# HGRN scores: the near halves of both directions in one 128x128 matmul per chunk, and the far half with doubled queries

## The chip, the cores and the metric

The kernel runs on one core of one Trainium2 chip. The metric is device time in microseconds (us) from start to end of one execution; lower is better. Five engines work side by side, each on its own list of instructions in order: PE (matmul, with its weight loads shown apart as PEld), DVE (vector operations), ACT (activation functions and copies), POOL and SP (which here issues the DMA transfers). They wait for one another through semaphores.

## The reference, cut to what matters

The reference is a two-layer backbone over 512 latent tokens and 256 context tokens of width 1024. Its first layer has a bidirectional HGRN2 mixer: a gated linear recurrence, run forward and backward, with 8 heads of 128 features. Within a chunk each direction computes scores between queries and keys, masked to what lies behind, and multiplies them with the values:

```python
b = jnp.cumsum(logf, axis=-2)
q_in = q * jnp.exp(b)
k_in = k * jnp.exp(-b)
scores = jnp.where(lower, jnp.einsum('nbhtd,nbhsd->nbhts', q_in, k_in), 0.0)
o_intra = jnp.einsum('nbhts,nbhse->nbhte', scores, v)
```

`f`, and so `b`, differs for the two directions; the backward direction is the same on flipped tokens. The two directions' outputs are added. The rest of the program (modulation, feed-forward halves, gated chunk MLP) is not touched by the change.

## The kernel before, in words

Weights stream from HBM in units of 128x1024; ACT and DVE split each into two parts (`split`, L95 on ACT and L96 on DVE, tile `w`), and each product of the large projections is three matmuls (L107, L108, L109). The units pass through buffers that come free as PE works on, so each split is released by PE's progress.

The HGRN stage loops over heads `h`, with the work on head `h - 1` put between the projections of head `h`. For each head PE makes: the forget projection of direction 0 (`psfl`, then `psfc` for the context tokens, L649 and L651), that of direction 1, the query projection `psq` of head `h`, and the gate projection `psq` of head `h - 1`. All of these are 24 matmuls of 512 or 256 columns. ACT and DVE turn each forget projection into the key tile `X` (Exp, Ln, Ln on ACT, L657 to L660; subtract, add, cumulative sum on DVE, L661 to L666; six references on L679; Exp on L680) and the decay tile `B` (L682, L683). The query projection goes through three ACT passes (L636 to L638) and one DVE product (L639). Then `queries` (L688) multiplies `B` of direction 0 and of direction 1 with the queries, one DVE instruction each: after it `B` is the query operand `Q` of that direction.

For head `h - 1` PE transposes keys (`ptk`, L694; ACT copies them to `kT`, L696), makes the states (`pkc`, `pkl`) and the scores. `scores` works on chunks of 128 tokens, keys on partitions, four chunks per direction. A 128x128 score block has a near half of 64 queries that see only 64 keys, and a far half of 64 queries that see all 128. So each chunk takes two matmuls: 64 keys by 64 queries (L707) and 128 keys by 64 queries (L708). DVE copies the allowed entries to the score tile `sT` with two predicated copies per direction (L711, L712). `outputs` adds the score tiles of the two directions (`ssum`, L760) and multiplies with the values (`po`, L764 to L766); the output is normalised (`on`), transposed (`pto`, L782), and multiplied with the gate.

The tile framework reorders instructions of one engine when it builds the program, so the order in the code is not exactly that of an engine; once built, each engine's order is fixed. Before the change the scores of direction 0 stand behind the next head's first forget projection and the transposes, those of direction 1 behind its second one.

Of the kernel before, what the change touches and what calls it, by code (L numbers as in the profile page):

```python
# [42 lines left out]
def backbone_kernel(  # L43
# [72 lines left out]
    def silu_row(pool, c):  # L116
        """silu of a conditioning vector, on every partition."""
        s = pool.tile([P, D], F32, name=f"srow_{c}")
        nc.sync.dma_start(s, cond[CI_OF[c]].partition_broadcast(P))
        nc.scalar.activation(s, s, AF.Silu)  # L120
        return s

    def mod_dot(pool, dst, w, s):
        """Sums of the halves of the products, so that no sum grows long."""
        n = D // 2
        for i in range(2):
            c = slice(i * n, (i + 1) * n)
            junk = pool.tile([P, n], BF16, tag="junk", name="junk", bufs=2)
            nc.vector.scalar_tensor_tensor(junk, w[:, c], 1.0, s[:, c], ALU.mult, ALU.mult, dst[:, i : i + 1])  # L129
# [63 lines left out]
    class OutPhase:  # L193
        """y = h @ w_out by token tiles, z = alpha x + gate y, its LayerNorm, and the next operand.

        x comes with its factor alpha, but for the first one (scaled=False)."""
# [45 lines left out]
        def store(self):  # L242
            """alpha times the LayerNorm's full result, for the next residual."""
# [40 lines left out]
        def operand(self, p, kb):  # L284
            """Two feature tiles of the next operand, for a pair of token tiles."""
# [88 lines left out]
    class Phase:  # L374
        """What the boundary before a phase may already start."""

        urgent, later = True, iter(())  # whether the residual's store is made at once, and what is put off
# [4 lines left out]
        @staticmethod  # L382
        def share(i, n):
            """Of n parts: two before the first operand step, the rest once the others are on their way."""
            return {0: range(2), 4: range(2, n)}.get(i, ())

        def ahead(self, i):
            """Work that needs nothing of this boundary, before its i-th operand step."""
# [4 lines left out]
    class FeedIn(Phase):  # L393
        """gate and up projections of a half-FFN, features on partitions."""
# [44 lines left out]
    class FeedContext(FeedIn):  # L439
        """The same of the context, whose operand is there before the latents'."""  # L440
# [15 lines left out]
    class HgrnValues(Phase):  # L456
        """First half of the token-major value projection, its latent tokens."""
# [33 lines left out]
    # ================= layer 0 =================  # L491
# [5 lines left out]
    with tc.tile_pool(name="hp", bufs=1) as hp, tc.tile_pool(name="modp", bufs=1) as modp:  # L497
        nc.scalar.preload_act_table(AF.Silu)
        srow = {"x": silu_row(modp, "x")}
        # x (1 + scale) + shift, features on partitions, a feature tile at a time  # L500
        f0 = FeedIn(0, 0, xm, NT, 6)
        with tc.tile_pool(name="first", bufs=1) as fp:
# [24 lines left out]
            for k in range(KD):  # L527
# [5 lines left out]
                # one feature tile behind, so that the next one's operand is on its way meanwhile  # L533
# [42 lines left out]
    with tc.tile_pool(name="hgo", bufs=1) as hgo:  # L576
        hts = [hgo.tile([P, 2, T], F32R, name=f"ht{h}") for h in range(NH)]
        with tc.tile_pool(name="hg", bufs=1) as hg:
# [37 lines left out]
            # values, tokens on partitions  # L616
# [13 lines left out]
            def proj_silu(h, idx, tag):  # L630
                """x sigmoid(x), the sigmoid as exp(-ln(1 + exp(-x)))."""
# [12 lines left out]

            def proj_forget(h, d):
                """Logit x: with e = exp(-x), f = (1 + lb e) / (1 + e) and 1 - f = (1 - lb) exp(-x) / (1 + e)."""
# [5 lines left out]
                r, i = Dir(), d * NH + h  # L652
                X = hg.tile([P, SEG * P], F32, tag="X", name="X", bufs=3)
                nc.vector.tensor_scalar(X[:, :T], ps, LOGIT_MIN, None, ALU.max)
                nc.vector.tensor_scalar(X[:, T:], psc[:, :TC], LOGIT_MIN, None, ALU.max)
                B = hg.tile([P, SEG * P], F32, tag="B", name="B", bufs=4)
# [6 lines left out]
                # cumulative log-decay within chunks; keys and queries relative to the middle of a latent  # L663
                # chunk, the keys of the context relative to the end of theirs
                st = 1 if d == 0 else -1
                nc.vector.tensor_tensor_scan(B[:, ::st], resets[d][:, ::st], B[:, ::st], 0.0, ALU.mult, ALU.add)  # L666
                B3 = B.rearrange("p (s t) -> p s t", t=P)
# [12 lines left out]
                nc.scalar.activation(X, X, AF.Exp, scale=-1.0, bias=lnoml[:, i : i + 1])  # L680
                Q = B3[:, :NT, :]
# [20 lines left out]
            def scores(d, r):  # L702
                """Masked scores, keys on partitions."""
                psc3 = bank("pssc").rearrange("p (s t) -> p s t", t=P)
                near, far = (slice(0, H), slice(H, P)) if d == 0 else (slice(H, P), slice(0, H))
                for s in range(NT):
                    nc.tensor.matmul(psc3[near, s, near], r.kk[:, s, near], r.Q[:, s, near], start=True, stop=True)  # L707
                    nc.tensor.matmul(psc3[:, s, far], r.kk[:, s, :], r.Q[:, s, far], start=True, stop=True)  # L708
                sT = sts[d]
                mk = mask[d].bitcast(I32).broadcast_to([P, NT, P])  # L710
                nc.vector.copy_predicated(sT[near], mk[near], psc3[near])  # L711
                nc.vector.copy_predicated(sT[far, :, far], mk[far, :, far], psc3[far, :, far])  # L712
# [22 lines left out]
            def latent_states(h, d, r, kT):  # L735
# [7 lines left out]
                for i, s in enumerate(order):  # L743
# [6 lines left out]
                    S1 = hg.tile([P, P], F32, tag="S1", name="S1", bufs=2)  # L750
# [42 lines left out]
            for h in range(NH + 1):  # L793
                if h < NH:
                    n0, last = proj_forget(h, 0)
                else:
                    op.lead(0, 1)
# [3 lines left out]
                if prev:  # L801
                    r0, r1 = prev
                    kTc = transposed([r.kk[:, NT + s, :] for r in prev for s in range(NTC)])
                    kT0 = transposed([r0.kk[:, s, :] for s in lat_order(0)[:-1]])
                    scores(0, r0)
# [4 lines left out]
                if prev:  # L810
# [3 lines left out]
                    scores(1, r1)  # L814
# [25 lines left out]
    with tc.tile_pool(name="hp2", bufs=1) as hp, tc.tile_pool(name="modp2", bufs=1) as modp, bpools() as bp:  # L840
# [16 lines left out]
        class GateIn(Phase):  # L857
            """Token-major half of the chunk MLP's projection, its first group."""
# [118 lines left out]
def _feature_units(w):  # L977
    """(D, n * 128) -> (n, 128, D // 128 * 128): features by 128, contraction rows on partitions."""
    k, n = w.shape
    return w.reshape(k // P, P, n // P, P).transpose(2, 1, 0, 3).reshape(n // P, P, k)  # L980


def _row_units(w, block):
    """(k, n) -> (n // block, k // 256, 128, 2 * block): two contraction tiles of a block of columns."""
# [67 lines left out]
```

## Time and profile before

| | |
|---|---|
| time, median of 3 runs | 2554.14 us (2553.33 to 2558.38) |
| span of the profiled execution | 2559.4 us, 5.3 us (0.2%) above that median |
| PE busy | 2511.2 us, 98% of the span |
| DVE, ACT busy | 1561.4 us (61%), 887.5 us (35%) |
| mean granted PE clock | 0.994 |
| first forget projection to last head's output | 642.5 to 973 us |

The page gives no time of the profiled execution beside its span, so sums are made against the span, and differences are carried over to the median. A row of the timeline has the start in us from the start of the span, the duration in us, the engine, the line, the operation, output and input tiles with their shapes, and how often the instruction follows itself; brackets hold the idle time of that engine just before, and what ended it. Matmuls overlap in the pipeline, so their cost in a stream is read from start to start, not from their durations. A row of the table by stretches has the stretch, its length, the busy time of each engine with its instruction count, then the granted PE clock (1.00 is full), the DMA share and the GB/s.

### The profile page before, as it was taken

Reading aid. Unit: us, or ns where it says so; the run is one execution under the profiler, and the core shown is the slowest. Engines: PE = TensorE matmul, PEld = TensorE weight load, DVE = VectorE, ACT = ScalarE, POOL = GpSimd, SP = SyncE. Lnnn points to the kernel's source line nnn. Section 1 sums busy time; section 2 is a strip of 40 time slices with the busy share of each in tenths; the row PEclk is TensorE's granted clock in tenths of the full one; section 3 lists DMA queues with packets and bytes.
Section 4 is the critical chain, followed back from the end, with each engine's and each line's share of the span. In section 5 each row is a group of like instructions: output and inputs, shape, how many; then the busy total and the mean of one; then the engine's idle time right before and its main releaser. Section 6 shows DMA issues by size and latency. Waiting matters only on the chain.

```text
span 2559.4 us, 32071 instructions
## 1 busy us (share of the span) xinstructions
PE 2511.2 (98%) x12591; PEld 2142.1 (84%) x12591; DVE 1561.4 (61%) x2773; ACT 887.5 (35%) x1210; POOL 45.1 (2%) x80
## 2 busy tenths in 40 slices
PE   7999999999999999999899999999999999999998
PEld 5888889988888888888678888888998888888887
DVE  7987568472888876766766522357467446632255
ACT  4222335462544433321233322343332233422232
POOL 0000000000000000000000000000000000000001
PEclk9999999999999999999999999999999999999999
DMA  8878326551211113788832522222533222432221
GB/s 324 294 260 279 128 95 227 191 188 50 75 65 52 50 58 116 263 289 275 268 127 87 181 99 97 93 95 96 191 124 105 82 99 91 172 109 98 99 91 58
DMA packets 111000, 367.18 MB, mean 143 GB/s; under 512 B 12744, under 2 KB 16000, under 8 KB 110848
## 3 DMA queue, kind: packets, MB, share of 16 engines
q1 hardware_dynamic: 110848, 365.13, 41.5%
q8 instruction: 98, 1.61, 0.3%
q14 instruction: 54, 0.44, 0.1%
HBM read 352.47 MB, written 12.61 MB: 143 GB/s over the span
## 4 chain that ended last, share of the span: by engine, by line
PE 85%; DMA 7%; DVE 5%; POOL 1%; issue 1%; ACT 0%; SPq 0%; DVEq 0%; POOLq 0%; ACTq 0%
PE psf L108 11%; PE psf L109 11%; PE psf L107 11%; PE y L107 8%; PE y L109 8%; PE y L108 8%; DMA mraw<-in_mod_w 7%; DVE junk L129 2%; PE pscv L109 2%; PE pscv L108 2%; PE pscu L108 2%; PE pscu L107 2%; PE pscu L109 2%; PE pscv L107 2%; PE psfl L107 1%; PE psq L109 1%
## 5 line engine op out<-in xcount | busy, mean ns | idle before, releaser
L96 DVE TENSOR_TENSOR w<-raw,w 128x1024 fp32r<-128x1024 f32 (+1 forms) x458 | 550.1, 1203 | 338.1 <-ACT w L95 335.5
L95 ACT ACTIVATE w<-raw 128x1024 fp32r<-128x1024 f32 (+1 forms) x458 | 473.1, 1039 | 437.7 <-PE psf L109 199.5
L107 PE MATMUL psf<-xm,w 128*128 128x512 f32 (+1 forms) x1504 | 566.8, 379 | 18.2 <-ACT xm L95 17.7
L108 PE MATMUL psf<-xm,w 128*128 128x512 f32 (+1 forms) x1504 | 568.7, 378 | 2.1 <-DVE xm L96 2.1
L109 PE MATMUL psf<-xm,w 128*128 128x512 f32 (+1 forms) x1504 | 568.0, 378 | 1.5 <-DVE w L96 1.5
L109 PE MATMUL y<-w,hs 128*128 128x512 f32 x984 | 387.4, 394 | 14.3 <-DVE hs L96 14.3
L107 PE MATMUL y<-w,hs 128*128 128x512 f32 x984 | 388.1, 394 | 0.0
L108 PE MATMUL y<-w,hs 128*128 128x512 f32 x984 | 387.5, 394 | 0.0
L107 PEld LDWEIGHTS psf<-xm,w 128*128 128x128 f32 x1504 | 284.2, 190 | 71.5 <-ACT xm L95 18.8
L108 PEld LDWEIGHTS psf<-xm,w 128*128 128x128 f32 x1504 | 286.0, 190 | 54.7 <-DVE xm L96 3.5
L109 PEld LDWEIGHTS psf<-xm,w 128*128 128x128 f32 x1504 | 285.9, 190 | 53.9 <-DVE w L96 2.9
L96 DVE TENSOR_TENSOR hs<-h,hs 128x512 fp32r<-128x512 f32 (+1 forms) x220 | 138.6, 636 | 170.4 <-ACT hs L95 170.2
L109 PEld LDWEIGHTS y<-w,hs 128*128 128x128 f32 x984 | 185.7, 189 | 56.3 <-DVE hs L96 14.8
L95 ACT ACTIVATE hs<-h 128x512 fp32r<-128x512 f32 (+1 forms) x220 | 129.1, 588 | 289.2 <-PE y L109 260.0
L129 DVE SCALAR_TENSOR_TENSOR junk<-mraw,srow_x 128x512 bf16<-128x512 f32 x256 | 167.5, 688 | 87.7 <-DMA mraw<-in_mod_w 87.0
L107 PEld LDWEIGHTS y<-w,hs 128*128 128x128 f32 x984 | 185.8, 189 | 41.9 <-ACT hs L95 0.2
L108 PEld LDWEIGHTS y<-w,hs 128*128 128x128 f32 x984 | 185.9, 189 | 40.6
L417 ACT ACTIVATE silu<-psf 128x512 f32<-128x512 f32 (+1 forms) x110 | 60.8, 552 | 424.2 <-PE psf L109 241.7
L419 DVE TENSOR_TENSOR h<-psf,silu 128x512 f32<-128x512 f32 (+1 forms) x110 | 69.7, 634 | 101.7 <-PE psf L109 99.7
L107 PE MATMUL psf<-xmc,w 128*128 128x256 f32 x352 | 99.8, 284 | 0.0
L109 PE MATMUL psf<-xmc,w 128*128 128x256 f32 x352 | 99.7, 283 | 0.0
L108 PE MATMUL psf<-xmc,w 128*128 128x256 f32 x352 | 99.7, 283 | 0.0
(202 smaller groups left out, 3216.4 us busy)
## 6 DMA issues: line engine op xcount, KB each, us to landing
raw<-in_ffn_w_in SPq DMA_DIRECT2D x220, 512.0 KB, 3.6
mraw<-in_mod_w SPq DMA_DIRECT2D x144, 512.0 KB, 4.5
raw<-in_ffn_w_out SPq DMA_DIRECT2D x110, 512.0 KB, 3.2
raw<-in_hg_wf SPq DMA_DIRECT2D x32, 512.0 KB, 3.2
raw<-in_cm_wv SPq DMA_DIRECT2D x32, 384.0 KB, 3.1
raw<-in_cm_wu SPq DMA_DIRECT2D x24, 512.0 KB, 3.3
raw<-in_cm_w_out SPq DMA_DIRECT2D x24, 512.0 KB, 3.2
x<-x SPq DMA_DIRECT2D x40, 256.0 KB, 2.4
```

The costliest lines, as they stand in the source:

```text
L95: nc.scalar.activation(dst_hi, src, AF.Copy)
L96: return nc.vector.tensor_tensor(dst_lo, src, dst_hi.bitcast(F32), ALU.subtract)
L107: nc.tensor.matmul(ps, ah, bh, start=start, stop=False)
L108: nc.tensor.matmul(ps, ah, bl, start=False, stop=False)
L109: return nc.tensor.matmul(ps, al, bh, start=False, stop=stop)
L129: nc.vector.scalar_tensor_tensor(junk, w[:, c], 1.0, s[:, c], ALU.mult, ALU.mult, dst[:, i : i + 1])
L417: nc.scalar.activation(s[:, :n], psg[:, :n], AF.Silu)
L419: nc.vector.tensor_tensor(h[:, :n], psu[:, :n], s[:, :n], ALU.mult)
```

## The change

The two tiles `B` of one head become one tile of two rows, so that one access pattern can take 64 queries of direction 0 and 64 of direction 1 for a chunk. The near keys of both directions are copied side by side into a new tile `kkn` (one ACT copy per direction). `near_scores` multiplies both at once, 128 keys by 128 queries; of its result the two diagonal blocks of 64x64 are used, one for each direction, with one predicated copy each. `far_scores` keeps 128 keys by the 64 far queries, but reads those queries twice, as 128 columns, and uses the first half of the result. `near_scores` is called at the start of the next head's turn, ahead of its first forget projection; `far_scores` stands where `scores` stood. Tile `S1` has one buffer instead of two.

```diff
+            both = {}
+
+            def pair():
+
+                both = hg.tile([P, 2, SEG * P], F32, tag="B", name="B", bufs=2)
+                rows = both[:, 0, :]
+                near = bass.AP(
+                    tensor=rows.tensor, offset=rows.offset,
+                    ap=[rows.ap[0], [SEG * P + H, 2], [P, NT], [1, H]],
+                )
+                kkn = hg.tile([P, NT, 2, H], F32, tag="kkn", name="kkn", bufs=1)
+                return (both[:, 0, :], both[:, 1, :]), near, kkn
+
             def proj_forget(h, d):
...
+                if d == 0:
+                    both[h] = pair()
...
-                B = hg.tile([P, SEG * P], F32, tag="B", name="B", bufs=4)
+                Bs, r.Qn, r.kkn = both[h]
+                B = Bs[d]
...
                 nc.scalar.activation(X, X, AF.Exp, scale=-1.0, bias=lnoml[:, i : i + 1])
+                near = slice(0, H) if d == 0 else slice(H, P)
+                nc.scalar.activation(r.kkn[:, :, d, :], X3[:, :NT, near], AF.Copy)
...
-            def scores(d, r):
...
-                psc3 = bank("pssc").rearrange("p (s t) -> p s t", t=P)
-                near, far = (slice(0, H), slice(H, P)) if d == 0 else (slice(H, P), slice(0, H))
+            def near_scores(r):
+
+                ps = bank("pssn").rearrange("p (s t) -> p s t", t=P)
                 for s in range(NT):
-                    nc.tensor.matmul(psc3[near, s, near], r.kk[:, s, near], r.Q[:, s, near], start=True, stop=True)
-                    nc.tensor.matmul(psc3[:, s, far], r.kk[:, s, :], r.Q[:, s, far], start=True, stop=True)
-                sT = sts[d]
+                    nc.tensor.matmul(ps[:, s, :], r.kkn[:, s].rearrange("p d t -> p (d t)"), r.Qn[:, :, s, :], start=True, stop=True)
+                for d, n in ((0, slice(0, H)), (1, slice(H, P))):
+                    mk = mask[d].bitcast(I32).broadcast_to([P, NT, P])
+                    nc.vector.copy_predicated(sts[d][n, :, n], mk[n, :, n], ps[n, :, n])
+
+            def far_scores(d, r):
+
+                ps = bank("pssc").rearrange("p (s i t) -> p s i t", i=2, t=H)
+                far = slice(H, P) if d == 0 else slice(0, H)
+                for s in range(NT):
+                    q = r.Q[:, s, far].unsqueeze(1).broadcast_to([P, 2, H])
+                    nc.tensor.matmul(ps[:, s], r.kk[:, s, :], q, start=True, stop=True)
                 mk = mask[d].bitcast(I32).broadcast_to([P, NT, P])
-                nc.vector.copy_predicated(sT[near], mk[near], psc3[near])
-                nc.vector.copy_predicated(sT[far, :, far], mk[far, :, far], psc3[far, :, far])
+                nc.vector.copy_predicated(sts[d][:, :, far], mk[:, :, far], ps[:, :, 0, :])
...
-                    S1 = hg.tile([P, P], F32, tag="S1", name="S1", bufs=2)
+                    S1 = hg.tile([P, P], F32, tag="S1", name="S1", bufs=1)
...
             for h in range(NH + 1):
+                if prev:
+                    r0, r1 = prev
+                    near_scores(r0)
...
-                    scores(0, r0)
+                    far_scores(0, r0)
...
-                    scores(1, r1)
+                    far_scores(1, r1)
```

The built program differs on PE, DVE and ACT. In the pieces below, taken from a head in the middle of the loop, the line numbers are those of the kernel named.

PE, where the gate projection (`psq`) ends and the next head's first forget projection (`psfl`) begins. Before:

```order
L107 MATMUL psq<-xm,w 128x512
L108 MATMUL psq<-xm,w 128x512
L109 MATMUL psq<-xm,w 128x512
L107 MATMUL psfl<-xm,w 128x512
L108 MATMUL psfl<-xm,w 128x512
L109 MATMUL psfl<-xm,w 128x512
```

The change:

```order
L107 MATMUL psq<-xm,w 128x512
L108 MATMUL psq<-xm,w 128x512
L109 MATMUL psq<-xm,w 128x512
L724 MATMUL pssn<-B,kkn 128x128 x4
L107 MATMUL psfl<-xm,w 128x512
L108 MATMUL psfl<-xm,w 128x512
L109 MATMUL psfl<-xm,w 128x512
```

The four near matmuls (`pssn`) stand between the two projections. For the first head there is no gate projection of an earlier head, and they stand right behind the query projection. The first `po` matmuls of `outputs` follow eight `psfl` matmuls later (ten before).

DVE, around the products with the queries: `q` is the query product, `S`, `Sc` and the numbered `S_` tiles belong to the recurrent states. Before, from the query product on:

```order
L639 TENSOR_TENSOR q<-psq,q 128x512
L752 SCALAR_TENSOR_TENSOR S<-pkl,se,S_7940 128x128
L688 TENSOR_TENSOR B<-B,q 128x512
L745 TENSOR_SCALAR Sc<-S,se 128x128
L751 TENSOR_SCALAR S_7946<-S,se 128x128
L688 TENSOR_TENSOR B<-B,q 128x512
L752 SCALAR_TENSOR_TENSOR S<-pkl,se,S_7946 128x128
L760 TENSOR_TENSOR ssum<-sT_5377,sT_5378 128x512
L745 TENSOR_SCALAR Sc<-S,se 128x128
L96 TENSOR_TENSOR w<-raw,w 128x1024
```

The change, from the sum of the score tiles on:

```order
L785 TENSOR_TENSOR ssum<-sT_5377,sT_5378 128x512
L770 TENSOR_SCALAR Sc<-S,se 128x128
L776 TENSOR_SCALAR S_7544<-S,se 128x128
L777 SCALAR_TENSOR_TENSOR S<-pkl,se,S_7544 128x128
L770 TENSOR_SCALAR Sc<-S,se 128x128 x2
L776 TENSOR_SCALAR S_7562<-S,se 128x128
L96 TENSOR_TENSOR w<-raw,w 128x1024
L777 SCALAR_TENSOR_TENSOR S<-pkl,se,S_7562 128x128
L639 TENSOR_TENSOR q<-psq,q 128x512
L770 TENSOR_SCALAR Sc<-S,se 128x128
L776 TENSOR_SCALAR S_7568<-S,se 128x128
L706 TENSOR_TENSOR B<-B,q 128x512
```

The sum `ssum` and one split of a weight unit (L96) moved from behind the two query products of `B` to ahead of `q`; the second product of `B` follows two rows later. The near halves' predicated copies (L727) stand some rows further on, behind the gate product.

ACT, where a forget projection is finished. Before:

```order
L675 ACTIVATE se<-sm 128x14
L680 ACTIVATE X<-X,lnoml 128x768
L683 ACTIVATE B<-B 128x512
L95 ACTIVATE w<-raw 128x1024
L657 ACTIVATE B<-X 128x768
```

The change:

```order
L691 ACTIVATE se<-sm 128x14
L696 ACTIVATE X<-X,lnoml 128x768
L701 ACTIVATE B<-B 128x512
L698 ACTIVATE kkn<-X 128x4x64
L95 ACTIVATE w<-raw 128x1024
L673 ACTIVATE B<-X 128x768
```

The copy into `kkn` stands ahead of the next weight split and of the next direction's first activation. The lists of SP and POOL have the same rows in the same order.

More of the change, by code (lines that the diff above doesn't have):

```diff
@@ L387, in ahead @@
         def ahead(self, i):
+            pass
         def staged(self, p, kb):
@@ L665, in proj_forget @@
                 st = 1 if d == 0 else -1
+                B3 = B.rearrange("p (s t) -> p s t", t=P)
                 nc.vector.tensor_tensor_scan(B[:, ::st], resets[d][:, ::st], B[:, ::st], 0.0, ALU.mult, ALU.add)
-                B3 = B.rearrange("p (s t) -> p s t", t=P)
                 X3 = X.rearrange("p (s t) -> p s t", t=P)
@@ L801, in backbone_kernel @@
                 if prev:
-                    r0, r1 = prev
                     kTc = transposed([r.kk[:, NT + s, :] for r in prev for s in range(NTC)])
                     kT0 = transposed([r0.kk[:, s, :] for s in lat_order(0)[:-1]])
-                    scores(0, r0)
+                    far_scores(0, r0)
                 if h == NH and 0 == 1:
```

## The prediction

> **What bounds the kernel now.** I read the page's first lines, then PE's waits in the HGRN stage, a table of two stretches of one head's turn, and the timeline of PE and DVE through that turn. The page, and PE's waits between 640 and 975 us (engine and line, what it waited for, total us, times, longest):
>
> ```profile
> span 2559.4 us, 32071 instructions
> PE 2511.2 (98%) x12591; PEld 2142.1 (84%) x12591; DVE 1561.4 (61%) x2773; ACT 887.5 (35%) x1210; POOL 45.1 (2%) x80
> ...
> PE pto L782 <- DVE on L776: 0.3, 1, 0.3
> ```
>
> So the stage is PE's alone: in 330 us it waits once, 0.3 us. But the share of DVE over the whole span hides this:
>
> ```profile
> 711.91:740.01 28.10, 28.10 (x164) 23.96 (x163) 26.27 (x63) 15.06 (x22) 0.00 (x0) 1.00 0.11 38
> 740.01:751.16 11.15, 11.15 (x74) 10.12 (x73) 6.17 (x12) 3.39 (x6) 1.02 (x1) 1.00 0.28 94
> ```
>
> In the first 28.10 us of a turn DVE is busy 26.27, in the last 11.15 us only 6.17. DVE runs almost without a pause through the two forget projections and the query products, and PE does not notice, because nothing on PE needs those products soon. I follow one turn, from DVE's clamp of one forget projection (L655 at 711.91) to the same clamp one head later (751.16): 39.25 us. PE starts the next head's first forget projection at 740.13.
>
> **What PE saves.** Start to start, three chunks of scores and three matmuls of 128x128 by 128 columns:
>
> ```profile
> 713.00 0.33 PE L707 MATMUL pssc<-B,X 128*64 128x64 f32 x2
> 713.26 0.43 PE L708 MATMUL pssc<-B,X 128*128 128x64 f32 x2
> ...
> 714.87 0.33 PE L707 MATMUL pssc<-B,X 128*64 128x64 f32 x2
> ...
> 742.40 0.38 PE L765 MATMUL po<-Sc,B 128*128 128x128 f32 x2
> ...
> 743.07 0.39 PE L765 MATMUL po<-Sc,B 128*128 128x128 f32 x2
> ```
>
> A chunk of scores takes (714.87 - 713.00) / 3 = 0.62 us, 0.26 for the 64-key and 0.37 for the 128-key matmul; a full matmul with twice the columns takes (743.07 - 742.40) / 3 = 0.22. The array's shape changes at every score matmul (128*64, 128*128) and never among the `po` ones, so I price every new score matmul at 0.22: its lower bound is this, its upper bound the 0.37 of L708, should the cost lie in the operands. Per head 8 x 0.62 = 5.0 us become 12 x 0.22 = 2.7: 2.3 us less, 18.6 us for 8 heads, if nothing else moves.
>
> **What the change makes PE wait for.** The four near matmuls stand at the point of 740.13, and they need the queries' products of both directions (the second L688). Rows of DVE, and PE's row there:
>
> ```profile
> 711.91 0.42 DVE L655 TENSOR_SCALAR X<-psfc 128x256 f32<-128x256 f32 x1 [2.15 <-PE psfc L109]
> 715.60 0.75 DVE L711 COPY_PREDICATED sT<-mask,pssc 64x512 f32<-64x512 int32 x1 [0.66 <-PE pssc L708]
> 717.20 0.45 DVE L712 COPY_PREDICATED sT<-mask,pssc 64x256 f32<-64x256 int32 x1
> 724.02 0.42 DVE L655 TENSOR_SCALAR X<-psfc 128x256 f32<-128x256 f32 x1 [0.34 <-PE psfc L109]
> 725.12 1.22 DVE L96 TENSOR_TENSOR w<-raw,w 128x1024 fp32r<-128x1024 f32 x1
> 726.25 0.34 DVE L729 SCALAR_TENSOR_TENSOR S<-S,se,pkc 128x128 f32<-128x128 f32 x1
> 727.04 0.96 DVE L662 TENSOR_TENSOR X<-X,L 128x768 f32<-128x768 f32 x1
> 734.05 0.76 DVE L711 COPY_PREDICATED sT<-mask,pssc 64x512 f32<-64x512 int32 x1
> 735.11 0.43 DVE L712 COPY_PREDICATED sT<-mask,pssc 64x256 f32<-64x256 int32 x1
> 739.33 0.68 DVE L688 TENSOR_TENSOR B<-B,q 128x512 f32<-128x512 f32 x1
> 740.20 0.68 DVE L760 TENSOR_TENSOR ssum<-sT,sT 128x512 f32<-128x512 f32 x1
> 740.79 0.28 DVE L745 TENSOR_SCALAR Sc<-S,se 128x128 f32<-128x128 f32 x1
> 740.99 1.22 DVE L96 TENSOR_TENSOR w<-raw,w 128x1024 fp32r<-128x1024 f32 x1
> 751.16 0.42 DVE L655 TENSOR_SCALAR X<-psfc 128x256 f32<-128x256 f32 x1 [2.16 <-PE psfc L109]
> ...
> 740.13 0.39 PE L107 MATMUL psfl<-xm,w 128*128 128x512 f32 x1
> ```
>
> Before, the second product ends at 739.33 + 0.68 = 740.01, when PE stands at 740.13, and its first reader comes over 10 us later. Now PE arrives earlier and DVE has to be there. The chain from L655 to the end of that product is 28.10 us. Its changes:
>
> First direction: DVE's wait for the scores (0.66) goes, since PE comes earlier, and the copies 0.75 + 0.45 become one like L712, 0.75 less. That would be 1.4, and with the 0.34 that DVE waited for `psfc` at 724.02 1.75. But L662 at 727.04 waits for ACT, and ACT now carries the copy into `kkn` ahead of its weight split and its first Exp. The nearest rows of a copy of 256 to 384 columns:
>
> ```profile
> L95 ACT ACTIVATE hs<-h 128x256 fp32r<-128x256 f32 x44 | 18.3, 417 | 21.0 <-PE y L109 19.1 <-DVE h L419 1.8
> L696 ACT ACTIVATE kT<-ptk 128x384 f32<-128x384 f32 x16 | 7.5, 471 | 2.7 <-PE ptk L694 2.7
> ```
>
> I take 0.4 us (bounds 0.3 and 0.6 for its strided rows), so L662 comes some 1.3 us sooner, not 1.75. Second direction: copies 0.76 + 0.43 become 0.44, 0.75 less. But the built order puts `ssum` (start to start 740.79 - 740.20 = 0.59) and a weight split (726.25 - 725.12 = 1.13) ahead of the query product, and two small state products (about 0.2 each) behind it: +1.3. Together -1.3 - 0.75 + 1.3: the chain takes 27.35 us, at best 26.9 if the copy is free and at worst 28 if it costs 0.6 in both directions.
>
> Then PE's part: four near matmuls, 4 x 0.22 = 0.9, and what lies between 740.13 and the clamp at 751.16, 11.05. The turn is 27.35 + 0.9 + 11.05 = **39.3 us**, against 39.25 before. By PE's work alone it would be 39.25 - 2.3 = 36.95. So PE waits about 2.4 us at the near matmuls of every turn (bounds 1.9 and 3.1), and the saving of that turn is gone: 7 turns, +0.5 us together. Nothing on PE can pass: the forget projection, and with it the whole next turn, is queued behind the near matmuls.
>
> The first head is worse. No gate projection lies between its query projection and the near matmuls:
>
> ```profile
> 664.60 0.39 PE L107 MATMUL psfl<-xm,w 128*128 128x512 f32 x1
> ...
> 672.19 1.28 DVE L688 TENSOR_TENSOR B<-B,q 128x512 f32<-128x512 f32 x2
> ```
>
> PE is done with the query projection at 664.60, the products are there at 673.47: a wait of 8.9 us, and 0.9 for the matmuls. Behind the last near matmuls there are only the two far ones: 2 x (4 x 0.62 - 4 x 0.22) = 3.2 us less. Sum with the PE clock as before: 8.9 + 0.9 + 0.5 - 3.2 = **+7 us**.
>
> **The clock.** PE is no longer busy throughout. What PE's earlier waits did to its granted clock (the number ahead of the last two columns of a stretch):
>
> ```profile
> 1395.14 0.74 PE L107 MATMUL psf<-xm,w 128*128 128x256 f32 x4 [1.42 <-ACT xm L95]
> 1762.77 0.44 PE L107 MATMUL pscv<-w,xm 128*128 128x384 f32 x1 [1.55 <-ACT xm L95]
> 2185.78 0.74 PE L107 MATMUL psf<-xm,w 128*128 128x256 f32 x4 [1.78 <-ACT xm L95]
> 1283.04 0.80 PE L109 MATMUL y<-w,hs 128*128 128x512 f32 x1 [14.32 <-DVE hs L96]
> ...
> 1393.40:1398.00 4.60, 2.87 (x22) 2.43 (x21) 4.23 (x10) 2.16 (x4) 0.79 (x2) 1.00 0.38 122
> 1765.00:1769.00 4.00, 3.77 (x24) 3.42 (x23) 3.42 (x7) 2.27 (x4) 0.79 (x2) 1.00 0.00 0
> 2186.80:2190.10 3.30, 3.28 (x15) 3.28 (x16) 2.93 (x6) 0.92 (x2) 0.79 (x2) 0.50 0.00 0
> 2190.30:2196.00 5.70, 5.70 (x51) 5.70 (x50) 4.45 (x7) 2.47 (x5) 0.00 (x0) 1.00 0.27 95
> 1283.00:1289.00 6.00, 5.96 (x14) 4.71 (x15) 5.97 (x15) 0.43 (x1) 0.00 (x0) 0.50 0.53 175
> ```
>
> Waits of 1.42 and 1.55 us left the clock at 1.00; one of 1.78 was followed by 3.3 us at 0.50, one of 14.32 by 6 us at 0.50 after PE had restarted. Half clock for 3.3 us loses 1.65 us of PE time, and right after the near matmuls PE sets the pace. A wait of 2.4 us is above 1.78: I charge six of the seven turns, 9.9 us, and 3.0 for the long first wait. Sum: 7 + 9.9 + 3.0 = 19.9, so **+20 us**: 2554.1 + 20 = 2574.
>
> The Trainium skill speaks against this term: its page TensorE: Matmul & The Clock Gate, in the section Why this matters for your kernels, warns only of idle gaps above about 3 us. By that rule the seven short waits would cost nothing and only the first one would slow the clock, the first rival below; the row of 1.78 us above disagrees with it, the rows of 1.42 and 1.55 do not.
>
> **Rivals.** (1) The clock holds in the short waits. The 1.78 us wait stood behind a run of transposes, which may not have counted as work, and the near matmuls stand behind full projections; against it, the wait of 1.55 us that left the clock alone had transposes ahead of it too. Then 7 + 3.0 = +10: 2564. (2) Faster: the products with the queries are in time. The mechanism is PE's bound holding as now: if DVE's early rows slip into pauses that I counted as work, the chain shortens; from 24.9 us on (27.35 - 2.4) PE no longer waits, a turn is 36.95 and seven save 16.1. Against it stands that DVE was busy for 26.27 us of the 28.10. With the first wait, 8.9 + 0.9 + 3.0 - 3.2 - 16.1 = -6.5: 2547.6. (3) The waits come out at 1.5 us, under those that touched the clock: turns of 38.4, 7 x 0.9 = 6.3 saved, 8.9 + 0.9 + 3.0 - 3.2 - 6.3 = +3: 2557. (4) Split or repeated queries are read no faster than L708's 0.37. Then near costs 8 x 4 x 0.15 = 4.8 more, all on the path, the last two far ones 1.2, and the far ones of the turns only fill PE's wait: +26, 2580.
>
> **How the numbers follow.** Forecast 0.55, rivals (1) 0.21, (2) 0.11, (3) 0.07, (4) 0.06. A measurement here tells about 0.2%, 5 us, from no change; so slower is the forecast with (1) and (4), 0.82; same is (3), 0.07; faster is (2), 0.11. The range runs from 2556, just under (3), to 2582: above (4), and 8 us above the forecast for a `kkn` copy of 0.6 us (7 x 0.6 = 4.2) and a seventh turn and a longer first spell at half clock. Left out are (2) and the tails.
>
> **What would show it.** In the profile after: PE waiting at L724 for DVE's L706, about 9 us once and 2 to 3 us seven times; turns of 39 us or, with the clock, 41, against 39.25; stretches at 0.50 behind these waits; the score matmuls 0.22 apart; `kkn` copies of 0.4 us. The forecast is wrong if PE does not wait at L724, wrong in its last term if the clock stays at 1.00 there, and wrong in its first if a near or far matmul takes 0.37.

## The result, and the profile after

The changed kernel takes 2579.67 us (median of 4 runs, 2575.51 to 2581.49) against 2556.26 us for the kernel before on the same chip: a ratio of 1.0087, with an interval of 1.0075 to 1.0100. It is slower, by 0.9%. The forecast was 2574 in a range of 2556 to 2582.

The page of the profile after, its first line and the engines' shares, then PE's waits between 640 and 1000 us (engine and line, what it waited for, total us, times, longest):

```profile
span 2579.7 us, 31948 instructions
...
PE 2504.1 (97%) x12527; PEld 2139.8 (83%) x12527; DVE 1555.8 (60%) x2773; ACT 890.9 (35%) x1226; POOL 45.2 (2%) x80
...
PE pssn L724 <- DVE B L706: 11.8, 5, 2.4
PE pssn L724 <- ACT kkn L698: 9.2, 1, 9.2
PE pssn L724 <- ACT g L637: 4.7, 2, 2.3
```

The span grew by 20.3 us (2559.4 before). PE is busy 7 us less and yet the kernel is longer: PE now waits 25.7 us at the near matmuls, once 9.2 us and seven times 2.3 to 2.4 us. Two of the seven are put down to the gate's ACT work and the first to the `kkn` copy. All eight end 0.15 to 0.2 us after DVE's second L706 of that head in the timeline, so I read them as one wait under three names.

Two turns of the changed kernel, in DVE's and PE's timeline (start, us, engine, line, operation; in brackets the idle time before it):

```profile
728.77 0.42 DVE L670 TENSOR_SCALAR X<-psfc 128x256 f32<-128x256 f32 x1 [2.18 <-PE psfc L109]
742.73 0.96 DVE L678 TENSOR_TENSOR X<-X,L 128x768 f32<-128x768 f32 x1
755.56 0.69 DVE L706 TENSOR_TENSOR B<-B,q 128x512 f32<-128x512 f32 x1
769.99 0.42 DVE L670 TENSOR_SCALAR X<-psfc 128x256 f32<-128x256 f32 x1 [2.18 <-PE psfc L109]
811.09 0.42 DVE L670 TENSOR_SCALAR X<-psfc 128x256 f32<-128x256 f32 x1 [2.18 <-PE psfc L109]
837.89 0.68 DVE L706 TENSOR_TENSOR B<-B,q 128x512 f32<-128x512 f32 x1
850.72 0.42 DVE L670 TENSOR_SCALAR X<-psfc 128x256 f32<-128x256 f32 x1 [2.18 <-PE psfc L109]
...
756.40 2.04 PE L724 MATMUL pssn<-B,kkn 128*128 128x128 f32 x8 [2.35 <-DVE B L706]
758.10 0.77 PE L107 MATMUL psfl<-xm,w 128*128 128x512 f32 x1
758.67 0.63 PE L108 MATMUL psfl<-xm,w 128*128 128x512 f32 x1
```

From the clamp (now L670) to the end of the second query product there are 755.56 + 0.69 - 728.77 = 27.48 us, and 27.48 again in the turn that begins at 811.09. PE starts 0.15 us after that product. The turn from 728.77 lasts 769.99 - 728.77 = 41.22 us, the one from 811.09 only 39.63. The difference is the clock. In the longer one, the near matmuls take from 756.40 to 758.10, 1.7 us in place of 0.9, and the projection behind them starts a matmul every 0.4 to 0.6 us in place of 0.23.

The granted clock behind the waits, from the table by stretches (the stretch, its length, busy time by engine, then the granted PE clock, DMA share and GB/s):

```profile
671.00:681.20 10.20, 5.76 (x18) 4.92 (x19) 5.09 (x14) 1.98 (x4) 0.00 (x0) 0.50 0.16 51
715.40:718.80 3.40, 3.40 (x13) 3.01 (x13) 2.99 (x7) 0.29 (x1) 0.00 (x0) 0.50 0.36 101
756.30:759.70 3.40, 3.30 (x12) 3.04 (x13) 3.33 (x8) 0.60 (x1) 0.00 (x0) 0.51 0.29 81
...
838.20:841.60 3.40, 2.88 (x17) 2.57 (x18) 3.39 (x9) 1.00 (x2) 0.00 (x0) 1.00 0.21 58
879.20:882.60 3.40, 3.40 (x11) 2.72 (x10) 2.36 (x6) 0.00 (x0) 0.00 (x0) 0.50 0.48 154
...
961.10:964.50 3.40, 3.40 (x13) 2.92 (x13) 2.88 (x6) 0.18 (x1) 0.00 (x0) 0.51 0.41 123
```

The two stretches left out, from 797.3 and from 920.2, are at 0.50 as well: six of the seven short waits are followed by 3.4 us at half clock. The one near 838 is not, and its turn is the one of 39.63 us.

The HGRN stage, from its first `psfl` matmul to its last `pto`, took 330.3 us before and takes 352.4 now, 22.1 us more, cut at the clamps of the first forget projection (the 8.5 us ahead of the first of these clamps are the same in both and left out):

| part of the stage | before, us | after, us | difference | by the prediction's terms |
|---|---|---|---|---|
| first turn, with the long wait | 23.00 | 35.24 | +12.2 | 8.9 + 0.9 + 3.0 = +12.8 |
| six turns | 234.1 | 245.5 | +11.3 | 6 x 0.07 + 5 x 1.65 = +8.7 |
| from the last head's clamp to the end | 64.65 | 63.21 | -1.4 | 0.07 + 1.65 - 3.2 = -1.5 |

### The profile page after: what moved, and what is told of

Its sections match the earlier page's. It is cut to its first block, busy times and chain, and to the rows that moved or that the text cites. A ratio compares the mean times of both kernels' runs of the same rounds, so it can differ in the third digit from the quotient of the medians.

```text
span 2579.7 us, 31948 instructions
## 1 busy us (share of the span) xinstructions
PE 2504.1 (97%) x12527; PEld 2139.8 (83%) x12527; DVE 1555.8 (60%) x2773; ACT 890.9 (35%) x1226; POOL 45.2 (2%) x80
## 4 chain that ended last, share of the span: by engine, by line
PE 68%; DVE 13%; DMA 12%; ACT 3%; issue 2%; POOL 1%; SPq 0%; DVEq 0%; POOLq 0%; ACTq 0%
DMA mraw<-in_mod_w 10%; PE psf L108 8%; PE psf L109 8%; PE psf L107 8%; PE y L107 8%; PE y L109 8%; PE y L108 8%; DVE junk L129 4%; PE pscv L109 2%; PE pscv L108 2%; PE pscu L108 2%; PE pscu L107 2%; PE pscu L109 2%; PE pscv L107 2%; DVE w L96 2%
## 5 line engine op out<-in xcount | busy, mean ns | idle before, releaser
L96 DVE TENSOR_TENSOR w<-raw,w 128x1024 fp32r<-128x1024 f32 (+1 forms) x458 | 550.4, 1204 | 345.2 <-ACT w L95 342.6
L96 DVE TENSOR_TENSOR hs<-h,hs 128x512 fp32r<-128x512 f32 (+1 forms) x220 | 138.6, 636 | 165.8 <-ACT hs L95 165.6
L107 PEld LDWEIGHTS y<-w,hs 128*128 128x128 f32 x984 | 185.4, 188 | 41.2
```

Source lines behind the costliest of these rows:

```text
L96: return nc.vector.tensor_tensor(dst_lo, src, dst_hi.bitcast(F32), ALU.subtract)
L107: nc.tensor.matmul(ps, ah, bh, start=start, stop=False)
```

## The experiments

The theory to test is that of the prediction: PE's saving is real, but a chain of work on DVE ends 2.4 us after PE arrives at the near matmuls, so the turn is set by that chain, and the wait then also costs clock.

### The near matmuls behind the forget projection

The near matmuls of a head are issued behind the next head's first forget projection, so that PE has some 9 us of other work between the query products and their first reader. For the last head, which no forget projection follows, they stand behind a piece of the output projection (`op.lead`). Nothing else is changed:

```diff
-            def proj_forget(h, d):
+            def proj_forget(h, d, between=None):
...
+                if between is not None:
+                    near_scores(between)
...
-                    near_scores(r0)
...
-                    n0, last = proj_forget(h, 0)
+                    n0, last = proj_forget(h, 0, r0 if prev else None)
                 else:
                     op.lead(0, 1)
+                    near_scores(r0)
```

> The changed kernel, with the four near matmuls moved behind the next head's first forget projection (8.4 us of PE work further on); nothing else differs. Theory A (the loss is PE's wait at the near matmuls, 9.2 us once and 2.3 us in seven turns, and the half clock behind them): the waits at the near matmuls go but for about 1 us at the first head, the clock stays at 1.00 in the stage, and of PE's saving of 18.6 us 12 to 18 show: 2538 to 2545 us, ratio about 0.994. Theory B (the added ACT copies, the moved DVE rows and the new access patterns cost the time, wherever the near matmuls stand): no faster than before, 2556 us or more. Theory C (the price of a chunk does not fall to 0.22 us per matmul): score matmuls more than 0.3 us apart and 2550 us or more.

Measured: 2545.63 us against 2557.52, ratio 0.9954 (0.9939 to 0.9969): the changed kernel's own matmuls, placed elsewhere, make the kernel faster, if by a little less than theory A's range. The granted clock stays at 1.00 throughout the stage. PE's waits in the stage, and its far block with the row behind it:

```profile
PE po L792 <- DVE Sc L772: 2.8, 7, 0.4
PE pssn L726 <- ACT w L95: 1.4, 1, 1.4
...
713.39 1.06 PE L737 MATMUL pssc<-B,X 128*128 128x128 f32 x8
714.20 0.48 PE L107 MATMUL psfl<-xm,w 128*128 128x512 f32 x1
```

The 25.7 us of waits at the near matmuls are gone but for one of 1.4, and a turn is 748.97 - 711.50 = 37.47 us by the clamps:

```profile
711.50 0.43 DVE L672 TENSOR_SCALAR X<-psfc 128x256 f32<-128x256 f32 x1 [0.20 <-PE psfc L109]
748.97 0.42 DVE L672 TENSOR_SCALAR X<-psfc 128x256 f32<-128x256 f32 x1 [0.21 <-PE psfc L109]
```

The bound by PE's work alone was priced at 36.95. What is missing, 0.5 us a turn, is mostly the new wait of `po` for the scaled states `Sc` (2.8 / 7 = 0.4): with PE faster, the next thing that DVE makes late is seen.

### Without the second reading of the far queries

The kernel above, with the 64 far queries read once:

```diff
-                    q = r.Q[:, s, far].unsqueeze(1).broadcast_to([P, 2, H])
-                    nc.tensor.matmul(ps[:, s], r.kk[:, s, :], q, start=True, stop=True)
+                    nc.tensor.matmul(ps[:, s, 0, :], r.kk[:, s, :], r.Q[:, s, far], start=True, stop=True)
```

> As the kernel with the late near matmuls, but the far half reads its 64 queries once (128 keys by 64 columns). If the price of the old far matmul (0.37 us) lies in the change of the array's shape between neighbouring matmuls: far matmuls about 0.22 us apart and the same time as with doubled queries, within 2 us. If it lies in the 64 columns: far matmuls 0.37 us apart, 64 x 0.15 = 9 us slower than with doubled queries.

Measured: 2541.33 us, ratio 0.9941 (0.9923 to 0.9958), 4 us under the kernel above, with intervals that overlap. The far block:

```profile
712.93 1.00 PE L736 MATMUL pssc<-B,X 128*128 128x64 f32 x8
713.74 0.48 PE L107 MATMUL psfl<-xm,w 128*128 128x512 f32 x1
```

It lasts 713.74 - 712.93 = 0.81 us with 64 columns and 714.20 - 713.39 = 0.81 with 128. Reading the queries twice buys nothing. What differs in the traces is the order: here two more `psfl` matmuls stand ahead of `po`, its wait for `Sc` does not appear, and a turn takes 37.0 us in place of 37.5, so the 4 us are not a price of the columns.

### Only the far queries doubled

The reverse, on the kernel before: two matmuls per chunk as ever, the far one with its queries read twice. Its results go to a bank of their own (`pssf`), and the predicated copies are cut to match; of the edit, the matmul:

```diff
-                    nc.tensor.matmul(psc3[:, s, far], r.kk[:, s, :], r.Q[:, s, far], start=True, stop=True)
+                    q = r.Q[:, s, far].unsqueeze(1).broadcast_to([P, 2, H])
+                    nc.tensor.matmul(psf4[:, s], r.kk[:, s, :], q, start=True, stop=True)
```

> The kernel before, with only the far half changed: its 64 queries are given twice as 128 columns (in a bank of its own), the near matmuls stay 64 keys by 64 queries beside them. If the price lies in the 64 columns of the far matmul: the chunk falls from 0.62 to 0.26 + 0.22 = 0.48 us, 64 x 0.14 = 9 us less, 2547 us. If it lies in the change of the array's shape between near and far: the chunk stays at 0.62 us or grows by the longer stream (up to 0.1), 2556 to 2563 us.

Measured: 2557.67 us against 2557.52, ratio 1.0003 (0.9994 to 1.0013). Chunks, start to start:

```profile
715.25 0.33 PE L708 MATMUL pssc<-B,X 128*64 128x64 f32 x2
715.51 0.49 PE L710 MATMUL pssf<-B,X 128*128 128x128 f32 x2
715.93 0.33 PE L708 MATMUL pssc<-B,X 128*64 128x64 f32 x2
```

A chunk takes 0.68 us, 0.06 more than before. So the far matmul's 0.37 us in the kernel before was neither its 64 columns nor its operands: the same matmul costs 0.2 among its like and 0.42 here, between matmuls of another array shape (128\*64 and 128\*128 in the rows).

### The scores in one array shape

If the change of shape is the price, the kernel before can shed it in two lines, without the new tiles, copies and places of the change. The same entries are cut the other way: 64 near keys against all 128 queries, then 64 far keys against the 64 far queries.

```diff
-                    nc.tensor.matmul(psc3[near, s, near], r.kk[:, s, near], r.Q[:, s, near], start=True, stop=True)
-                    nc.tensor.matmul(psc3[:, s, far], r.kk[:, s, :], r.Q[:, s, far], start=True, stop=True)
+                    nc.tensor.matmul(psc3[near, s, :], r.kk[:, s, near], r.Q[:, s, :], start=True, stop=True)
+                    nc.tensor.matmul(psc3[far, s, far], r.kk[:, s, far], r.Q[:, s, far], start=True, stop=True)
```

> The kernel before, with the same score entries cut the other way: per chunk and direction the 64 near keys against all 128 queries, then the 64 far keys against the 64 far queries. Both matmuls have 64 keys, so the array keeps its 128x64 shape within a direction; no key copies, no doubled queries, order and waits as before. Theory (the 0.62 us of a chunk was the price of changing the array's shape at every score matmul): a chunk takes 0.22 + 0.11 to 0.22, 0.33 to 0.45 us, 64 x 0.2 to 0.3 = 11 to 18 us of PE work less, of which some 0.4 us per turn come back as waits for the states: 2540 to 2547, ratio 0.993 to 0.997. Rival (moving from one half of the array to the other, or 64-column operands as such, are the price): a chunk stays at 0.55 to 0.65 and the time within 3 us of the kernel before.

Measured: 2540.90 us against 2553.83 (5 and 9 runs), ratio 0.9945 (0.9932 to 0.9958). It beats the kernel before and the changed one, and equals the best above. Four chunks of one direction, and the matmul behind them:

```profile
711.51 0.32 PE L707 MATMUL pssc<-B,X 128*64 128x128 f32 x1
711.52 0.33 PE L708 MATMUL pssc<-B,X 128*64 128x64 f32 x2
...
712.22 0.38 PE L707 MATMUL pssc<-B,X 128*64 128x128 f32 x2
712.53 0.50 PE L107 MATMUL psfl<-xm,w 128*128 128x512 f32 x1
```

The block lasts 712.53 - 711.51 = 1.02 us. In the kernel before, the four chunks at 0.62 took 2.5. The stage of the profiled execution is 19 us shorter (311.2 in place of 330.3), the medians are 13 apart; the profiled execution of the kernel before lay 5 us above its median. The block is shorter than I expected (0.33 to 0.45 a chunk; it is 0.25), and the starts show why: L707 and L708 start within 0.02 us of each other through the block, so the matmuls of the two halves of the array run side by side. The Trainium skill has both halves of this, in its page TensorEngine Tiling (Array Packing), section Tiling Modes: changing the tiling mode drains the engine, changing only the tile does not, and different tiles run in parallel. The page gives no price. Here a far matmul between others of another shape took 0.2 us more than among its like, and a block that keeps its shape and uses both halves at once took 1.5 us less.

### PE kept busy in the wait

Nine matmuls of 512 columns on operands long there, with results that are overwritten, stand ahead of the near matmuls in six turns. Nothing needs them:

```diff
+                for _ in range(fill):
+                    nc.tensor.matmul(pb, xm[:, 0, 0, 0:P], xm[:, 0, 0, :], start=True, stop=True)
...
-                    near_scores(r0)
+                    near_scores(r0, 9 if 1 < h < NH else 0)
```

> The changed kernel, with nine matmuls of 512 columns on operands that lie ready, put directly ahead of the near matmuls of turns 2 to 7 (six turns; they write the bank that the near matmuls then overwrite, 9 x 0.23 = 2.1 us). PE is busy there instead of waiting. If the wait alone sets the turn (39.3 us) and the clock is what makes it 41: the clock stays at 1.00 behind those six turns, each saves up to 1.7 us, 8 to 10 us less than the changed kernel, 2569 to 2572 us, although PE has more to do. If the clock does not follow PE's idle time, or the turn is 41 us for another reason: no less than the changed kernel's 2580, and up to 2 us more.

Measured: 2573.39 us against 2557.52, ratio 1.0067 (1.0052 to 1.0082), and a span of 2569.3, 10 us under that of the changed kernel although PE has 54 matmuls more, 12 us of work. The medians say 7.5 us, a little less than expected: 15.9 above the kernel before in place of 23.4. (The profiled execution was the shortest of the four here and the longest of the four there.) One of the waits that is filled, and the stretch behind it:

```profile
750.74 2.20 PE L724 MATMUL pssn<-xm 128*128 128x512 f32 x9
753.23 1.13 PE L727 MATMUL pssn<-B,kkn 128*128 128x128 f32 x8 [0.29 <-ACT g L637]
...
752.70:756.10 3.40, 3.10 (x19) 2.32 (x18) 3.39 (x9) 1.02 (x2) 0.00 (x0) 1.00 0.18 59
```

The clock stays at 1.00 in all six turns, and they take 39.7 to 39.9 us in place of 41.1 to 41.2. So about 1.4 us of a turn was the clock, not the wait itself; the rest of the loss stays, as the chain on DVE is as long as it was (27.46 us). The one turn of the changed kernel at full clock took 39.63, 0.2 less than these: here PE needs 12.23 us from the near matmuls to the next clamp in place of 12.00.

### Four fill matmuls in place of nine

```diff
-                    near_scores(r0, 9 if 1 < h < NH else 0)
+                    near_scores(r0, 4 if 1 < h < NH else 0)
```

> The fill kernel with four fill matmuls instead of nine in the same six turns; the built order puts the first three matmuls of the next forget projection ahead of the near ones as well. That takes 5 x 0.23 = 1.15 us of PE work out of each turn and puts 0.7 us of needed work in front of the wait. Theory (the chain on DVE sets when the near matmuls run): the turn only loses the 0.7 us that moved in front, 39.1 us, with a wait of 0.7 to 1.0 us that leaves the clock at 1.00; about 2568, ratio 1.005. Rival (PE sets the pace): 38.7 us and no wait, 2566. Rival for the clock (waits under 1 us slow it too): stretches at 0.50 in those turns, 2575 or more.

Measured: 2565.66 us against 2555.93, ratio 1.0037 (1.0023 to 1.0051). A turn of it, with PE's rows at the near matmuls:

```profile
725.03 0.42 DVE L670 TENSOR_SCALAR X<-psfc 128x256 f32<-128x256 f32 x1 [1.91 <-PE psfc L109]
751.82 0.68 DVE L706 TENSOR_TENSOR B<-B,q 128x512 f32<-128x512 f32 x1
763.97 0.42 DVE L670 TENSOR_SCALAR X<-psfc 128x256 f32<-128x256 f32 x1 [1.92 <-PE psfc L109]
...
751.50 0.39 PE L109 MATMUL psfl<-xm,w 128*128 128x512 f32 x1
752.64 1.13 PE L727 MATMUL pssn<-B,kkn 128*128 128x128 f32 x8 [0.76 <-DVE B L706]
```

The chain is 751.82 + 0.68 - 725.03 = 27.47 us, PE waits 0.76 for it with the clock at 1.00, and the turn is 38.94 us: 27.47 + 0.14 + 11.33. The wait that the theory foresaw is there (0.7 to 1.0), and the rival's turn of 38.7 without a wait is not; the total alone, 2565.66, would not have told the two apart. Against 39.63, the changed kernel's turn at full clock, three needed matmuls in front of the wait are worth their full 0.7 us. The trace is that of the shortest of five executions, 2559.05 us; the other four took 2564.89 to 2566.30 at a mean granted clock of 0.992 to 0.993 in place of 0.995, and no trace shows where they lost it. That a wait of 0.76 leaves the clock alone is shown for this execution only.

### More work on DVE, twice

First, the fill kernel with every far predicated copy issued twice:

```diff
                 nc.vector.copy_predicated(sts[d][:, :, far], mk[:, :, far], ps[:, :, 0, :])
+                nc.vector.copy_predicated(sts[d][:, :, far], mk[:, :, far], ps[:, :, 0, :])
```

> The kernel with nine fill matmuls ahead of the near ones, with each far predicated copy of DVE issued twice (the second writes the same values): 2 x 0.36 to 0.44, about 0.8 us more DVE work per turn between the clamp and the products with the queries. Theory (the turn is set by DVE's chain from the clamp to the second query product, and the near matmuls wait for it): the chain takes 0.8 us longer, the wait at the near matmuls grows from 0.3 to about 1.0 us, turns go from 39.8 to 40.5, and the time is 4 to 6 us above that of the fill kernel, about 2578. Rival (PE's own work sets the pace, DVE only happens to end near it): turns stay within 0.2 us and the time within 2 us of the fill kernel, 2572 to 2575.

Measured: 2572.19 us against 2553.83, ratio 1.0071 (1.0056 to 1.0086): the same as the fill kernel, 1.0067. By its total this speaks for the rival. But DVE's rows show that it was no test of the chain:

```profile
725.75 0.42 DVE L670 TENSOR_SCALAR X<-psfc 128x256 f32<-128x256 f32 x1 [2.18 <-PE psfc L109]
729.91 0.44 DVE L741 COPY_PREDICATED sT<-mask,pssc 128x256 f32<-128x256 int32 x1
752.53 0.69 DVE L706 TENSOR_TENSOR B<-B,q 128x512 f32<-128x512 f32 x1
```

The chain still takes 752.53 + 0.69 - 725.75 = 27.47 us. The extra copy at 729.91 fell into DVE's pause of 0.33 us for ACT, and for that of the second direction the framework put one small state product behind the query products that had stood ahead of them. Added work is not an added link.

So, second, a link that nothing can pass: each query product is followed by a copy of its tile onto itself.

```diff
                 nc.vector.tensor_tensor(r.Q, r.Q, q.rearrange("p (s t) -> p s t", t=P), ALU.mult)
+                nc.vector.tensor_copy(r.Q, r.Q)
```

> The kernel with nine fill matmuls ahead of the near ones, with a link added to DVE's chain itself: each product with the queries is followed by a copy of its tile onto itself, 128x512, which the near matmuls must wait for (values unchanged; 0.35 to 0.7 us each, two per turn, and one pair of small state products comes to stand ahead of the second). Theory (near matmuls wait for the end of DVE's chain): the chain grows by 0.7 to 1.8 us, the wait at the near matmuls from 0.3 to between 1.0 and 2.1 us, turns from 39.8 to between 40.5 and 41.6, the time 4 to 11 us above the fill kernel: ratio to the kernel before 1.008 to 1.011. Rival (PE's own work sets the pace, as the doubled far copies seemed to say): turns and ratio as in the fill kernel, 39.8 and 1.007.

Measured: 2573.69 us against 2555.93, ratio 1.0064 (1.0048 to 1.0080). Again the total did not move. The rows:

```profile
726.74 0.42 DVE L670 TENSOR_SCALAR X<-psfc 128x256 f32<-128x256 f32 x1 [2.18 <-PE psfc L109]
755.12 0.42 DVE L707 COPY B<-B 128x512 f32<-128x512 f32 x1
766.77 0.42 DVE L670 TENSOR_SCALAR X<-psfc 128x256 f32<-128x256 f32 x1 [2.18 <-PE psfc L109]
...
754.57 0.39 PE L107 MATMUL psfl<-xm,w 128*128 128x512 f32 x1
755.69 0.46 PE L728 MATMUL pssn<-B,kkn 128*128 128x128 f32 x2 [0.73 <-DVE B L707]
```

This time the chain did grow, to 755.12 + 0.42 - 726.74 = 28.80 us, 1.33 more, and the wait at the near matmuls grew from 0.29 to 0.73. But in the built order four `psfl` matmuls now stand ahead of the near ones, 0.9 us of needed work that runs before the wait, and three of the four near matmuls come only behind `po`; the turn is 40.03 us in place of 39.8. With the chain, the 0.15 us to PE's start and 11.08 to the next clamp, it is again a sum of links. My expectation of the total failed, since I had taken PE's order as fixed; that the first near matmul starts when DVE's chain ends holds.

### The control: the same copies where PE has slack

The doubled far copies, in the kernel with the near matmuls late and the far queries read once:

> The kernel with the near matmuls behind the forget projection and the far queries read once, with each far predicated copy of DVE issued twice: the same 0.8 us of DVE work per turn as in the kernel that has it in the fill version. Theory (DVE sets the pace only where PE waits for the products at once): here PE has 11 us between the products and their first reader, so turns stay at 37.0 to 37.3 and the time at 2541 to 2544. Rival (with PE's work shorter, DVE's work as such bounds every order): turns grow by 0.8 and the time by about 6 us, to 2547.

Measured: 2542.50 us, ratio 0.9957 (0.9944 to 0.9971). A turn by its clamps:

```profile
713.60 0.41 DVE L672 TENSOR_SCALAR X<-psfc 128x256 f32<-128x256 f32 x1
750.75 0.42 DVE L672 TENSOR_SCALAR X<-psfc 128x256 f32<-128x256 f32 x1
```

It takes 750.75 - 713.60 = 37.15 us, against 37.0 without the second copies. DVE's work as such bounds nothing in this order. As the first of the pair above turned out to be no test of the chain, this control alone says little more than that.

## Why the prediction was right, point by point

**What PE saves.** I priced a score matmul of 128 columns at 0.22 us and put the 0.62 of a chunk down to the change of the array's shape. Both stand: the far block of the changed order is 0.81 us for four, the near block at full clock 0.88, the doubled queries alone left a chunk at 0.68, and the same entries in one shape took 1.02 in place of 2.5 for four chunks. Rival (4), matmuls of 0.37 us, is out. A turn by PE's work alone was put at 36.95 us, and with the near matmuls late and the far queries read once it takes 37.0. What I did not ask is whether the far matmuls needed the 128 columns; they do not.

**The wait in the turns.** The chain was forecast at 27.35 us and is 27.48, and its parts came out too: the subtraction of the second direction (L662, now L678 at 742.73) comes 1.2 us sooner behind the clamp (13.96 us in place of 15.13; 1.3 forecast), and the rest takes 0.55 more (13.52 in place of 12.97; 0.55 forecast); the wait at 2.4 (1.9 to 3.1) and is 2.3 to 2.4; a turn at full clock at 39.3 and the one there is takes 39.63, of which 0.15 is PE's start behind the product, a link that the sum left out. The `kkn` copy was priced at 0.4 and takes it, in each of its 16 instances:

```profile
L698 ACT ACTIVATE kkn<-X x16: 399/400/403, 662.9 to 954.5; 128x256 f32<-128x256 f32 x16
```

That the wait is the cause of the loss is shown by the kernel that only places the near matmuls later: from 0.9% slower to 0.5% faster. Rival (2), the products in time, and rival (3), waits of 1.5 us, are out.

**The first head.** Forecast 8.9 us of waiting and 0.9 for the matmuls, with 3.0 more for the clock. The wait is 9.2, and of the 10.2 us at 0.50 PE was busy 5.76, which loses 2.9. The three terms make 12.8; the first turn grew by 12.2.

**The clock.** I charged six of the seven waits with 1.65 us each, and six of the seven were followed by 3.4 us at 0.50. That the clock is a cost of its own is shown by the fill: same chain, clock at 1.00, turns 1.4 us shorter. The forecast was lucky in the count, as nothing in the trace of before told six from seven; and the trace after is one execution of four, with mean granted clocks of 0.989 to 0.991, so the count may differ from one to the next. The rule of the Trainium skill that I set against this term (TensorE: Matmul & The Clock Gate, in Why this matters for your kernels: gaps above about 3 us) would have led to rival (1); gaps of 2.3 to 2.4 us were enough here, so the measurement decides against it.

**What was mis-sized.** The six turns grew by 11.3 us where the terms make 8.7. I took 39.25 us for all turns before, but the first of the six was 37.91: PE had less work in it, but DVE's chain, which now sets the turn, is there as long as elsewhere (27.33 us), so that turn pays 1.3 us more. The other 1.3 is the balance of two: a turn at full clock is 39.63, some 0.3 above the sum (PE's start 0.15 us behind the product, and a chain longer by 0.13), 1.9 us in six turns, and a drop of the clock cost 1.5 us (41.1 to 41.2 against 39.63) in place of 1.65, 0.6 us less in five. Outside the stage the profiled execution was 1.8 us shorter, so that the span differs by 20.3, near the forecast's 20. The medians, 23.4 us apart, lie a little above.

## What to carry to other kernels

An engine that is busy 98% of the time can stand next to one that is just in time: before a consumer is moved forward, follow the producer's chain through the very stretch in which it is needed, since here a saving of 2.3 us a turn became a wait of 2.4 us, and the wait cost clock on top. The same matmuls behind one more projection kept most of the gain. And when a small matmul costs more than its size, look first at what stands beside it: keeping one array shape through a block, two lines of code, gave as much as the whole restructuring in its better place.

## What the hardware showed that I had not expected

**Two halves of the array side by side.** Matmuls of 64 keys, one in each half, started within 0.02 us of each other, and a chunk took 0.25 us; with the starts, that is read as running at the same time; I had expected them one behind the other, 0.33 us a chunk or more.

**The clock falls by a grid.** The six drops begin at 715.4, 756.3, 797.3, 879.2, 920.2 and 961.1 us: 41.0 us apart, or twice that across the turn without one. Turns without a drop would take 39.6 us; with it they take 41.1 to 41.2, so that each next wait meets the clock's window at about the same place. The Trainium skill's page TensorE: Matmul & The Clock Gate (What's actually happening) says that the window is 3.413 us and free-running; 12 of them are 40.96 us, and the trace agrees with that spacing, and with the 3.4 us that a drop lasts. Why the wait at 836.4 to 838.7 caused no drop I can only argue: by this grid a window ended at 838.3, with less of the wait inside it (1.9 us) than at 756.3 (2.2). Nor did a wait of 2.34 us ahead of the last near matmuls slow the fill kernel, where a wait of 1.78 us had slowed the kernel before elsewhere. The same wait in the fill kernel with doubled far copies was followed by half clock. The rows of the two, the fill kernel first:

```profile
952.43 1.13 PE L727 MATMUL pssn<-B,kkn 128*128 128x128 f32 x8 [2.34 <-DVE B L706]
952.10 2.05 PE L727 MATMUL pssn<-B,kkn 128*128 128x128 f32 x8 [2.34 <-DVE B L706]
```

Between 952.8 and 954.5 us the clock is 1.00 in the first and 0.50 in the second. So the length of a wait alone does not decide; that its place against the clock's window does is likely, but not shown. No run here sets the length from which a wait costs clock; the waits of 0.7 to 0.8 us in the kernel with four fill matmuls and in the one with longer products did not, in the executions traced.

**No price for 64 columns more.** Four far matmuls took 0.81 us with 64 columns and with 128.
